# A decoder layer on one core: all four pooling groups computed ahead of the attention, and the output projection of the first 256 tokens placed inside the last head pair

## The chip, the cores and the metric

One core of one Trainium2 chip runs the whole layer. The metric is the device time of one execution in microseconds. Three executions of the kernel before took 1055.33, 1055.5 and 1056.11 us; the median is 1055.5 us.

## The reference

One layer over 1024 tokens (S) of width 1024 (D), all in float32. `h = x @ w_in` gives four pooling groups of 128 columns, queries, keys and values of eight heads of 64 columns, and eight forget logits.

```
pool = scale * GroupLinear(TrailingMean_w(u) - u)     w = 2, 4, 8, 16 for the four groups
attn = causal softmax(q k / 8 + c_t - c_s) v          c = cumsum(log sigmoid(f + b_f))
x    = LayerNorm(alpha * x + concat(pool, attn) @ w_out)
x    = LayerNorm(alpha * x + relu(x @ w_mlp1)^2 @ w_mlp2)
```

## The kernel before, in words

**Precision.** Every float32 matrix is split into a rounded part "hi" and a remainder "lo" (`split`: line 71 is the cast on ScalarE, line 72 the subtraction on VectorE), and a product is three matmuls, hi*hi, hi*lo and lo*hi (`three`, lines 83 to 85). "Fill" below means matmuls of lines 83 to 85 of 512 columns.

**Stages.** Values and forget logits of all tokens; the pooling groups 3, 2, 1 (`EARLY`), whose projection is 48 fill matmuls each (`pool_group`), with 6 more in `pool_linear`; keys and queries of head pair 0 (`qk_proj`); then the attention, four pairs of heads; then the output projection and first LayerNorm of eight blocks t of 128 tokens; then the MLP, written as block products over quarters of the tokens (line 575, second matrix line 918).

**Attention.** A unit is (pair p, head e, token block m of 256 queries). `att_probs` makes scores in PSUM (lines 339, 340, and 342 for the mask), takes their running minimum with the gate row on VectorE (line 345) and the exponential on ScalarE (line 347). `att_values` transposes the probabilities on TensorE (line 368), splits each transposed tile (369 on ScalarE, 370 on VectorE), multiplies by the values (384), and joins the two halves (389 on ScalarE, 390 on VectorE). The result goes to `mix_dram` in HBM, unnormalised; `row_scales` (lines 399 to 404) sends the reciprocal row sums to `rin_dram`. The values of a unit are issued behind the scores of the next one.

**Fill inside the attention.** Between these steps `fillstep` issues pieces of three fill matmuls: in pairs 0 to 2 the projection of the next pair's keys and queries (96 matmuls), in pair 3 pooling group 0 (`LATE`, 54 matmuls). In pair 3 the units run by m, both heads for each, so that the first tokens are complete early.

**Output projection.** For each m the mixture is loaded back in two halves (pooling columns, attention columns), the second half is multiplied by the broadcast reciprocals (line 725), both are split; 48 matmuls make each block t, all eight k-tiles for columns 0 to 511 first, then for the rest. The norm runs on VectorE (`Norm.on_vector`), with one Sqrt on ScalarE (line 498). The normalised block is transposed (line 551) one block later.

**What sets the order.** Each engine runs its own list in order; the framework's scheduler writes these lists from the program and may move an instruction past others that it does not depend on. Buffers are slots of five tags (S 3, U 2, B 14, Q 10, A 9), and PSUM has banks s 3, pt 2, pv 1, mm 2. All loads and most stores go through the SP queue in order.

Of the kernel before, what the change touches and what calls it, by code (L numbers as in the profile page):

```python
# [8 lines left out]
F32 = mybir.dt.float32  # L9
# [3 lines left out]
ALU = mybir.AluOpType  # L13
# [16 lines left out]
EPS = 1e-5  # L30
MASK = -1e30
BIG = 3e38
EARLY, LATE = (3, 2, 1), (0,)


@with_exitstack
def trunk(ctx, tc, xT, xn, wuqk, wvf, bf, poolw, pscale, wout, g1, b1, w1, w2, g2, b2, out):
# [198 lines left out]
    def run(gen):  # L236
        for _ in gen:
            pass
# [29 lines left out]
    def pool_linear(g, slots):  # L268
        st = slot("S", [P], F32)
        nc.sync.dma_start(st, poolw[:, g])  # L270
        pw = slot("U", [2, P])
        split(pw[:, 0], pw[:, 1], st)
        dh, dl = pooled[g]
        mx = slot(slots, [S], F32)
        for c in range(NCH):
            cs = slice(c * CH, (c + 1) * CH)
            dst = bank("mm" if g in LATE else None)
# [4 lines left out]
    for g in EARLY:  # L282
        run(pool_group(g, None, "A"))
        if g == EARLY[0]:
            gate_sum(neglog)


# [118 lines left out]
    g0 = qk_proj(0)  # L406
    for _ in range(2 * KT):
        next(g0)
    pool_linear(EARLY[0], "A")
    run(g0)  # L410

    def last_fill():
        for g in LATE:
            yield from pool_group(g, "mm")
            pool_linear(g, "Q")

    fill = {"gen": iter(()), "credit": 0.0, "rate": 0.0}

    def fillstep():
        fill["credit"] += fill["rate"]  # L420
        while fill["credit"] >= 1.0:
            fill["credit"] -= 1.0
            next(fill["gen"], None)

    pend = None
    for p in range(NPAIR):
        if p + 1 < NPAIR:
            order = [(p, e, m) for e in range(2) for m in range(4)]
            gen, pieces, over = qk_proj(p + 1, "mm"), 4 * KT + 1, 28
        else:  # L430
            order = [(p, e, m) for m in range(4) for e in range(2)]
            gen, pieces, over = last_fill(), (2 * KT + 2) * len(LATE), 14
        fill.update(gen=gen, credit=0.0, rate=pieces / over)
        for unit in order:
            prob = att_probs(*unit)
            if pend is None:
                for g in EARLY[1:]:
                    pool_linear(g, "A")
            fillstep()
            if pend is not None:  # L440
                att_values(*pend)
            pend = (*unit, prob)
        run(gen)
    att_values(*pend)

    x1_dram = dr.tile([NT, P, D], F32, name="x1_dram")


    hid_dram = dr.tile([NF // 2, P, 2, 7 * CH], F32, name="hid_dram")
    H = KT // 2
    GROUPS = (("A12", "A11"), ("S1", "S2"), ("S3", "S4"), ("A22",))  # L460
    AT = {g[0]: 2 * i * CH for i, g in enumerate(GROUPS)}

    def quarters(a):
        return a.rearrange("p (q t) -> p q t", q=4)

    wo = []
    for kp in range(KT // 2):
        hi, lo = slot("B", [2, D]), slot("B", [2, D])
        for k in range(2):
            st = slot("S", [D], F32)  # L470
            nc.sync.dma_start(st, wout[2 * kp + k])
            split(hi[:, k], lo[:, k], st)
            wo.append((hi[:, k], lo[:, k]))

    def load_row(tag, src):
        t = slot(tag, [D], F32)
        nc.sync.dma_start(t, src.to_broadcast([P, D]))
        return t

    class Norm:  # L480

# [54 lines left out]
    gam, bet = load_row("Q", g1), load_row("Q", b1)  # L536
    A = {b: (slot("B", [H, CH]), slot("B", [H, CH])) for b in ("A11", "A12")}
    R0, R1, A22, raw22 = {}, {}, {}, {}

# [172 lines left out]
    NU = NF // 2  # L712
    units = [Unit(u) for u in range(NU)]
    last = None
    for m in range(4):
        mh = []
        for half in range(2):
            mf = slot("S", [4, 256], F32)
            nc.sync.dma_start(mf, mix_dram[m, :, 4 * half : 4 * half + 4, :])
            if half:  # L720
                rb = slot("S", [NPAIR, 256], F32)
                for e in range(2):
                    rows = rin_dram[e::2, m * 256 : (m + 1) * 256].rearrange("(o p) t -> o p t", o=1)
                    nc.sync.dma_start(rb[e * HD : (e + 1) * HD], rows.to_broadcast([HD, NPAIR, 256]))
                nc.vector.tensor_tensor(mf, mf, rb, ALU.mult)
            hi, lo = slot("Q", [4, 256]), slot("Q", [4, 256])
            split(hi, lo, mf)
            mh.append((hi, lo))
        for t in (2 * m, 2 * m + 1):
            ts_ = slice((t % 2) * P, (t % 2 + 1) * P)  # L730
# [10 lines left out]
            for n, part in enumerate(yp):  # L741
                ns = slice(n * CH, (n + 1) * CH)
                for k in range(KT):
                    a = mh[k // 4]
                    three(part, (a[0][:, k % 4, ts_], a[1][:, k % 4, ts_]), (wo[k][0][:, ns], wo[k][1][:, ns]), k == 0, k == KT - 1)
            if last is not None:
                x1_transposed(*last)
            nm = Norm(xt, gam, bet, x1_dram[t])
            for i, c in enumerate(nm.cols):
                nc.vector.scalar_tensor_tensor(xt[:, c], xt[:, c], ALPHA, yp[i], ALU.mult, ALU.add)  # L750
                nm.stats(i)
            nm.on_vector()
            last = (t, xt)

    def block(name, src):
# [55 lines left out]
    VERSIONS = ("B11", "B21", "T2", "T1", "T3", "B22", "T4")  # L811
    c0, c1 = slice(0, CH), slice(CH, D)
    tt = nc.vector.tensor_tensor
    y, k3s, t2b, rows = {}, {}, {}, {}

    class Pair:
# [188 lines left out]
    for i, x in enumerate(chain):  # L1005
        if isinstance(x, Unit):
            if x.u >= 4:
                at(i - 1, 0, x.load_f)
                at(i - 1, 2, x.load_g)
                at(i - 1, 3, x.split_f)  # L1010
                at(i - 1, 4, x.sums)
                at(i - 1, 6, x.split_t2)
            if x.u >= 3:
                at(i, 1, x.split_t14)
                at(i, 4, x.split_t3b)
            if x.kept is None:
                at(i + 1, 7, x.sums_s)
                at(i + 2, 1, x.out_r)
                at(i + 2, 2, x.out_s)
            else:  # L1020
                at(i + 1, 5, x.out_a)
                at(i + 1, 6, x.sums_s, x.out_r)
                at(i + 1, 7, x.out_s)
        else:
            for k, p in enumerate(p for p in pairs if FIRST[p.u] == x.s):
                if p.u == ORDER[0]:
                    at(i - 2, 1, p.load_f)
                    at(i - 2, 2, lambda p=p: p.load_g("Q"))
                else:
                    at(i - 1, 4 * k, p.load_f)  # L1030
                    at(i - 1, 2 + 3 * k, p.load_g)
                at(i - 1, 3 + 3 * k, p.split_b)
                at(i - 1 + k, 4 - 3 * k, p.sums)
                at(i - 1 + k, 5 - 4 * k, p.split_t2)
                at(i, 2 + k, p.split_t13)
                at(i, 6, p.split_t4b)
            if x.first:
                at(i - 1, 4, x.room)
            if 5 <= x.s < 13:
                at(i - 1, 6, x.load_x)  # L1040
                at(i, 4, x.add_x)
            for n, place in enumerate((-4, -1, 0, 2) if 2 <= x.s < 5 else (-2, 0, 2, 4)):
                at(i + (place < 0) * -1, place % 7, lambda x=x, n=n: x.load(GROUPS[n]))
            if x.s == NS - 5:
                at(i + 1, 0, lambda: rows.update(gb=(load_row("S", g2), load_row("S", b2))))
    at(1, 1, second.out_s)

    def places(i, n):
# [59 lines left out]
```

## Time and profile before

| | |
|---|---|
| median of three executions | 1055.5 us |
| the profiled execution | 1056.57 us, of which the span of its instructions 1054.8 us |
| TensorE / VectorE / ScalarE busy | 97% / 72% / 49% of the span |
| granted TensorE clock, mean | 0.991 |

A TensorE row of the profile counts an instruction from its start to its modelled end, and consecutive ones overlap; what a matmul costs in a stream is the distance from one start to the next. So a TensorE that is shown as busy may still be slower than its stream rate, and the comparison that helps is of a stretch's length with the number of its matmuls times that distance. Times inside the trace are counted from the start of the span.

### The profile page before, as it was taken

How to read it: one execution, taken by the hardware profiler on the slowest of the kernel's cores; microseconds unless marked ns; L12 is line 12 of the kernel's file. 1: busy time of each engine (PE TensorE's matmuls, PEld its weight loads, DVE VectorE, ACT ScalarE, POOL GpSimd, SP SyncE). 2: the span in 40 equal slices, each digit the busy share in tenths (PEclk: the TensorE clock that was granted, in tenths of full speed). 3: DMA queues.
4: the chain of work that ended last, by engine and by line, in shares of the span. 5: the costliest groups of instructions: out<-in, count | busy, mean ns of one | idle time of the engine just before them, and what ended most of it. 6: DMA issues, size and time to landing. Idle time of an engine off the chain costs nothing.

```text
span 1054.8 us, 14034 instructions
## 1 busy us (share of the span) xinstructions
PE 1023.5 (97%) x5006; PEld 847.5 (80%) x5006; DVE 761.3 (72%) x1297; ACT 513.6 (49%) x822; POOL 119.0 (11%) x187
## 2 busy tenths in 40 slices
PE   8999999999989999899999999999999999999995
PEld 8988787888768878688888888888788888888883
DVE  4576678676896798869878878788875566566446
ACT  4423565565773322567676666777621221122153
POOL 0000000000000021212212112120100000000056
PEclk9999999999999999899999999999999999999997
DMA  6202311111445542138756757665999888868753
GB/s 221 103 27 90 115 50 31 31 53 49 130 153 165 180 160 80 42 118 320 287 211 265 267 214 279 230 245 205 325 321 311 286 263 288 271 202 277 232 185 120
DMA packets 111510, 195.28 MB, mean 185 GB/s; under 512 B 9224, under 2 KB 77640, under 8 KB 111440
## 3 DMA queue, kind: packets, MB, share of 16 engines
q1 hardware_dynamic: 95456, 136.19, 39.5%
q0 software_dynamic: 15984, 58.20, 14.3%
q8 instruction: 39, 0.64, 0.3%
q14 instruction: 31, 0.25, 0.1%
HBM read 126.65 MB, written 67.70 MB: 184 GB/s over the span
## 4 chain that ended last, share of the span: by engine, by line
PE 83%; DVE 7%; DMA 4%; ACT 3%; issue 2%; SPq 0%; DVEq 0%; ACTq 0%
PE s L918 15%; PE s L575 12%; PE pv L918 8%; PE mm L575 7%; PE pt L575 6%; PE pv L575 4%; PE pv L384 3%; PE mm L85 2%; PE mm L83 2%; DMA S<-rin_dram 2%; PE mm L84 2%; PE s L83 2%; PE s L85 2%; PE s L84 2%; PE pt L918 2%
## 5 line engine op out<-in xcount | busy, mean ns | idle before, releaser
L71 ACT CAST B<-S 128x1024 fp32r<-128x1024 f32 (+1 forms) x92 | 78.5, 870 | 175.8 <-DMA S<-in_w_dram 70.3
L575 PE MATMUL s<-B,Q 128*128 128x512 f32 x504 | 121.8, 395 | 0.4 <-ACT B L71 0.4
L72 DVE TENSOR_TENSOR B<-S,B 128x1024 fp32r<-128x1024 f32 (+1 forms) x92 | 90.4, 994 | 39.8 <-ACT B L71 39.5
L575 PEld LDWEIGHTS s<-B,Q 128*128 128x128 f32 x504 | 96.2, 191 | 21.5 <-ACT B L71 0.9
L918 PE MATMUL s<-B,Q 128*128 128x512 f32 x399 | 96.9, 389 | 0.0
L71 ACT CAST Q<-S 128x1024 fp32r<-128x1024 f32 x53 | 55.6, 1051 | 66.8 <-PE s L575 17.9
L918 PEld LDWEIGHTS s<-B,Q 128*128 128x128 f32 x399 | 74.9, 188 | 15.6
L918 PE MATMUL s<-B,A 128*128 128x512 f32 x333 | 83.3, 395 | 3.8 <-DVE rt L499 2.2
L72 DVE TENSOR_TENSOR Q<-S,Q 128x1024 fp32r<-128x1024 f32 x53 | 64.6, 1221 | 25.7 <-ACT Q L71 25.5
L918 PEld LDWEIGHTS s<-B,A 128*128 128x128 f32 x333 | 62.6, 189 | 18.7 <-DVE rt L499 2.6
L575 PE MATMUL mm<-B,Q 128*128 128x512 f32 x324 | 77.6, 389 | 0.0
L693 POOL DMA_DIRECT2D hid_dram<-A x90 | 48.4, 543 | 233.9 <-ACT A L690 198.5
L575 PEld LDWEIGHTS mm<-B,Q 128*128 128x128 f32 x324 | 60.7, 188 | 12.9 <-DVE Q L72 0.4
L575 PE MATMUL pt<-B,Q 128*128 128x512 f32 x288 | 68.7, 389 | 0.0
L384 PE MATMUL pv<-A,B 128*128 128x256 f32 x320 | 61.6, 297 | 5.1 <-ACT A L369 3.3
L384 PEld LDWEIGHTS pv<-A,B 128*128 128x128 f32 x320 | 49.1, 188 | 21.4 <-ACT A L369 9.9
L575 PEld LDWEIGHTS pt<-B,Q 128*128 128x128 f32 x288 | 54.0, 188 | 11.2
L370 DVE TENSOR_TENSOR A<-pt,A 128x512 fp32r<-128x512 f32 (+1 forms) x80 | 49.2, 634 | 16.4 <-ACT A L369 15.8
L347 ACT ACTIVATE A<-A,nm 128x128 f32<-128x128 f32 (+3 forms) x64 | 49.8, 778 | 20.7 <-DVE nm L345 20.4
L691 DVE TENSOR_TENSOR A<-A,A 128x1024 f32<-128x1024 f32 x45 | 53.4, 1218 | 0.0
L83 PE MATMUL mm<-B,B 128*128 128x512 f32 x120 | 51.7, 431 | 0.0
L918 PE MATMUL pv<-B,Q 128*128 128x512 f32 x204 | 50.1, 389 | 0.0
(397 smaller groups left out, 2250.1 us busy)
## 6 DMA issues: line engine op xcount, KB each, us to landing
hid_dram<-A POOLq DMA_DIRECT2D x105, 512.0 KB, 4.0
S<-in_w_dram SPq DMA_DIRECT2D x62, 512.0 KB
Q<-hid_dram SPq DMA_DIRECT2D x104, 256.0 KB
A<-hid_dram SPq DMA_DIRECT2D x76, 256.0 KB
S<-in_wuqk_dram SPq DMA_DIRECT2D x12, 512.0 KB
A<-ncf_dram SPq DMA_DIRECT2D x8, 512.0 KB
S<-in_wout_dram SPq DMA_DIRECT2D x8, 512.0 KB
S<-mix_dram SPq DMA_DIRECT2D x8, 512.0 KB
```

Of the source, the lines that this page charges most:

```text
L71: nc.scalar.copy(hi, src)
L72: nc.vector.tensor_tensor(lo, src, hi.bitcast(F32), ALU.subtract)
L83: nc.tensor.matmul(dst, a[0], b[0], start=first, stop=False)
L84: nc.tensor.matmul(dst, a[0], b[1], start=False, stop=False)
L85: nc.tensor.matmul(dst, a[1], b[0], start=False, stop=last)
L347: nc.scalar.activation(pt[:, :nk], pt[:, :nk], AF.Exp, bias=nm, scale=-1.0, accum_out=rsum[h][:, i : i + 1])
L370: nc.vector.tensor_tensor(tt[:, 1, ev], tp[:, ev], tt[:, 0, ev].bitcast(F32), ALU.subtract)
L384: nc.tensor.matmul(ov, V[j][:, h].rearrange("p s d -> p (s d)"), tt[:, s, a:b], start=(j == 0 and s == 0), stop=(j == 2 * m + 1 and s == 1),)
L575: nc.tensor.matmul(dst, b[x][:, k], A[a][y][:, k], start=first and k == 0 and i == 0, stop=k == H - 1 and i == 2, skip_group_check=not first,)
L691: nc.vector.tensor_tensor(x, x, hi.bitcast(F32), ALU.subtract)
L693: nc.gpsimd.dma_start(hid_dram[self.u, :, i, AT[name] : AT[name] + 2 * CH], part.rearrange("p q n t -> p (q n t)"))
L918: nc.tensor.matmul(dst, h[:, p_], w[q_], start=first and u == self.us[0] and j == 0, stop=u == self.us[-1] and j == 2, skip_group_check=no ...
```

## The change

`GROUPED` replaces `EARLY` and `LATE`: all four pooling groups are projected ahead of the attention; the small products of groups 3 and 2 stand inside `qk_proj(0)`, those of 1 and 0 in the first unit. In pair 3 the fill is now the output projection of blocks t = 0 and 1 (96 matmuls and two norms). The output weights (`wo`), the norm's rows and the two x blocks take the B slots that the transposed input frees in pair 2. For every block the order is now half by half: pooling columns for both 512-column results, then attention columns for both.

```
-EARLY, LATE = (3, 2, 1), (0,)
+GROUPED = (3, 2, 1, 0)
...
+    def out_rows(t, yp):
+        ts_ = slice((t % 2) * P, (t % 2 + 1) * P)
+        for half in range(2):
+            for n, part in enumerate(yp):
+                for k in range(4):
...
+                    three(part, (a[0][:, k, ts_], a[1][:, k, ts_]), (w[0][:, ns], w[1][:, ns]), half + k == 0, half + k == 4)
+                    yield
...
+    def last_fill():
+
+        for t in range(2):
+            yp = [bank("mm") for n in range(2)]
+            yield from out_rows(t, yp)
+            first_norm(t, x01[t], yp)
...
-            gen, pieces, over = last_fill(), (2 * KT + 2) * len(LATE), 14
+            gen, pieces, over = last_fill(), 4 * KT + 2, 23
+            load_wo(0)
+            mixed(0, 0)
+            load_wo(1)
+            gb, x01 = slot("B", [2, D], F32), slot("B", [2, D], F32)
...
+                if pend[:3] == (NPAIR - 2, 1, 3):
+                    load_wo(2)
+                if pend[:3] == (NPAIR - 1, 0, 0):
+                    load_wo(3)
+                if pend[:3] == (NPAIR - 1, 1, 0):
+                    mixed(0, 1)
...
-    for m in range(4):
-        mh = []
+    x1_transposed(0, x01[0])
+    last = (1, x01[1])
+    for m in range(1, 4):
         for half in range(2):
...
+            mixed(m, half)
...
-                for un in units[:2]:
+                for un, tag in zip(units, ("B", "Q")):
                     un.load_f()
-                    un.split_f("B")
+                    un.split_f(tag)
```

`mixed(m, half)` and `load_wo(kp)` hold the loads and splits that stood inline before; `first_norm` holds the residual sum, the statistics and the norm.

Three places in the order. First TensorE in pair 3 of the kernel before, where its fill runs out: mm_3011 is pooling group 0, pt_3170 and pv_3169 belong to unit (3,1,1), pt_3261 to (3,0,2), the s tiles are scores.

```order
L84 MATMUL mm_3011<-B_415,B_2893 128x512
L85 MATMUL mm_3011<-B_415,B_2893 128x512
L368 MATMUL pt_3170<-ident_63,A_3076 128x128
L339 MATMUL s_3159<-Q_2283,Q_2284 128x256
...
L384 MATMUL pv_3169<-A_3179,B_379 128x256 x2
L401 MATMUL pt_3229<-ident_63,ri_3227 2x128
L384 MATMUL pv_3169<-A_3179,B_379 128x256 x2
L368 MATMUL pt_3261<-ident_63,A_3140 128x128
```

From there to the middle of unit (3,0,3) only six fill matmuls follow. The same place in TensorE's list of the change: mm_3100 is the second result of block t = 0, pt_3164 belongs to unit (3,1,0), pv_3222 to (3,0,1), pv_3373 to (3,0,2).

```order
L85 MATMUL mm_3100<-B_2975,Q_2972 128x512
L368 MATMUL pt_3164<-ident_63,A_3091 128x128
...
L384 MATMUL pv_3222<-A_3232,B_379 128x256 x2
L368 MATMUL pt_3297<-ident_63,A_3200 128x128
...
L83 MATMUL mm_3099<-B_3070,Q_3196 128x512
L84 MATMUL mm_3099<-B_3071,Q_3196 128x512
L83 MATMUL mm_3100<-B_3070,Q_3196 128x512
L84 MATMUL mm_3100<-B_3071,Q_3196 128x512
L384 MATMUL pv_3373<-A_3419,B_445 128x256 x2
L401 MATMUL pt_3449<-ident_63,ri_3447 2x128
L85 MATMUL mm_3099<-B_3070,Q_3197 128x512
```

The 24 fill matmuls of the pooling half of t = 0 come first; then none, from unit (3,1,0) to the end of (3,0,2); then Q_3196 and Q_3197, the attention half of the mixture, are there, and 38 stand nearly in a block. Last, ScalarE's list of the change behind that point: rt_3392 is the norm of t = 0, pt_3487 and pt_3495 are transposed probabilities of unit (3,1,2), A_3546 are scores of (3,1,3).

```order
L71 CAST Q_3763<-S_3757 128x1024
L431 ACT_TABLE_LOAD
L431 ACTIVATE rt_3392<-mv_3391,eps_77 128x1
L369 CAST A_3488<-pt_3487 128x512
L369 CAST A_3496<-pt_3495 128x512
...
L403 COPY row_3543<-pt_3541 2x128
L347 ACT_TABLE_LOAD
L347 ACTIVATE A_3546,rsum_3081<-A_3546,nm_3556 128x896
```

Before, one table load stood behind the last exponential; now the Sqrt of t = 0 lies between exponentials and that of t = 1 behind the last, so there are three table loads in place of one.

## Rows read from the trace of the kernel before

**Rows 1.** Busy time by stretch: start:end, length, busy us (instructions) of each engine, PEclk, DMA
```profile
50.00:100.00 50.00, 50.00 (x246) 42.09 (x245) 34.77 (x73) 13.47 (x23) 0.00 (x0) 1.00 0.17 58
...
165.00:218.00 53.00, 52.45 (x317) 42.80 (x316) 39.54 (x95) 33.38 (x73) 2.50 (x8) 1.00 0.14 41
...
271.00:294.00 23.00, 22.53 (x133) 17.91 (x132) 19.59 (x46) 17.20 (x41) 1.25 (x4) 1.00 0.46 150
294.00:318.00 24.00, 19.59 (x128) 15.74 (x126) 21.76 (x55) 19.92 (x39) 0.94 (x3) 1.00 0.47 149
318.00:330.00 12.00, 11.17 (x68) 9.52 (x68) 8.98 (x12) 6.17 (x13) 0.31 (x1) 1.00 0.51 144
...
366.00:371.00 5.00, 4.13 (x21) 3.19 (x19) 4.50 (x10) 3.51 (x6) 0.00 (x0) 1.00 0.00 2
```
**Rows 2.** TensorE's groups in pair 1, 165 to 218: shape, count, busy, mean ns
```profile
L384 PE MATMUL pv<-A,B 128*128 128x256 f32 x80 | 14.9, 297 | 0.5 <-ACT A L369 0.3
L83 PE MATMUL mm<-B,B 128*128 128x512 f32 x32 | 13.9, 435 | 0.0
```
**Rows 3.** TensorE's groups from 271 to 330
```profile
L384 PE MATMUL pv<-A,B 128*128 128x256 f32 x96 | 18.8, 301 | 3.6 <-ACT A L369 2.4 <-DVE U L390 0.7 <-DVE A L370 0.2
L368 PE MATMUL pt<-ident,A 128*128 128x128 f32 x86 | 12.9, 274 | 0.9 <-ACT row L403 0.9
L83 PE MATMUL mm<-B,B 128*128 128x512 f32 x15 | 6.5, 431 | 0.0
...
L83 PE MATMUL s<-B,Q 128*128 128x512 f32 x9 | 3.7, 415 | 0.1
```
**Rows 4.** Chain that ended last: start, us, what; streams of matmuls at full rate
```profile
168.95 0.44 PE pt L368 x4
169.39 0.47 PE pv L384 x4
...
419.20 2.75 PE s L575 x12
```
**Rows 5.** TensorE's timeline: start, us, instruction, idle time before it and what ended it
```profile
301.73 0.47 PE L339 MATMUL s<-Q,Q 128*128 128x512 f32 x1 [1.02 <-DVE nm L345]
...
315.62 0.50 PE L384 MATMUL pv<-A,B 128*128 128x256 f32 x2 [1.13 <-ACT A L369]
...
370.63 0.63 PE L551 MATMUL pv<-ident,A 128*128 128x128 f32 x4 [0.87 <-DVE A L516]
```
**Rows 6.** VectorE's groups by shape, 272 to 325
```profile
L72 DVE TENSOR_TENSOR B<-S,B 128x1024 fp32r<-128x1024 f32 x8 | 9.7, 1216 | 2.1 <-ACT B L71 2.0
L370 DVE TENSOR_TENSOR A<-pt,A 128x512 fp32r<-128x512 f32 x13 | 8.6, 685 | 1.0 <-ACT A L369 1.0
L345 DVE CUSTOM_DVE_ANT_0 A<-s,A 128x512 f32<-128x512 f32 x10 | 6.8, 684 | 0.3 <-issue 0.2
...
L725 DVE TENSOR_TENSOR S<-S,S 128x1024 f32<-128x1024 f32 x1 | 1.2, 1225 | 1.2 <-DMA S<-rin_dram 1.2
```
**Rows 7.** VectorE's timeline: one norm of a block
```profile
406.58 0.69 DVE L750 SCALAR_TENSOR_TENSOR A<-A,pt 128x512 f32<-128x512 f32 x1 [2.62 <-PE pt L85]
...
409.77 2.43 DVE L513 SCALAR_TENSOR_TENSOR A<-A,mv,Q 128x512 f32<-128x512 f32 x2
...
412.82 1.42 DVE L516 SCALAR_TENSOR_TENSOR A<-A,rt,Q 128x512 f32<-128x512 f32 x2
```
**Rows 8.** ScalarE's timeline: the one table load behind the attention
```profile
339.14 1.05 ACT L71 CAST Q<-S 128x1024 fp32r<-128x1024 f32 x1 [9.42 <-DVE S L725]
340.20 1.28 ACT L498 ACT_TABLE_LOAD   x1
341.71 0.29 ACT L498 ACTIVATE rt<-mv,eps 128x1 f32<-128x1 f32 x1 [0.22 <-DVE mv L495]
```
**Rows 9.** Chain that ended last: loads of the broadcast reciprocals, issue to landing
```profile
315.70 5.84 DMA S<-rin_dram
...
330.94 6.81 DMA S<-rin_dram
```

More of the change, by code (lines that the diff above doesn't have):

```diff
@@ L280, in pool_linear @@
         nc.sync.dma_start(mix_dram[:, :, g, :].rearrange("m p t -> p m t"), mx.rearrange("p (m t) -> p m t", m=4))
-    for g in EARLY:
+    for g in GROUPED:
         run(pool_group(g, None, "A"))
-        if g == EARLY[0]:
+        if g == GROUPED[0]:
             gate_sum(neglog)
@@ L408, in trunk @@
         next(g0)
-    pool_linear(EARLY[0], "A")
+    for g in GROUPED[:2]:
+        pool_linear(g, "A")
     run(g0)
[L412 to L431, printed above, removed]
-            gen, pieces, over = last_fill(), (2 * KT + 2) * len(LATE), 14
[L433 to L478, printed above, removed]
     class Norm:
@@ L534, in affine, with load_row, load_wo, mixed @@
             eng.dma_start(self.store, self.y)
-    gam, bet = load_row("Q", g1), load_row("Q", b1)
+    wo, mh = [], {}
+    def load_row(dst, src):
+        nc.sync.dma_start(dst, src.to_broadcast([P, D]))
+    def load_wo(kp):
+        hi, lo = slot("B", [2, D]), slot("B", [2, D])
+        for k in range(2):
+            st = slot("S", [D], F32)
+            nc.sync.dma_start(st, wout[2 * kp + k])
+            split(hi[:, k], lo[:, k], st)
+            wo.append((hi[:, k], lo[:, k]))
+    def mixed(m, half):
+        mf = slot("S", [4, 256], F32)
+        nc.sync.dma_start(mf, mix_dram[m, :, 4 * half : 4 * half + 4, :])
+        if half:
+            rb = slot("S", [NPAIR, 256], F32)
+            for e in range(2):
+                rows = rin_dram[e::2, m * 256 : (m + 1) * 256].rearrange("(o p) t -> o p t", o=1)
+                nc.sync.dma_start(rb[e * HD : (e + 1) * HD], rows.to_broadcast([HD, NPAIR, 256]))
+            nc.vector.tensor_tensor(mf, mf, rb, ALU.mult)
+        hi, lo = slot("Q", [4, 256]), slot("Q", [4, 256])
+        split(hi, lo, mf)
+        mh[m, half] = hi, lo
@@ new lines, in trunk, with fillstep @@
+    x1_dram = dr.tile([NT, P, D], F32, name="x1_dram")
+    x01 = []
+    def last_fill():
[3 more added lines that the diff above has]
+            first_norm(t, x01[t], yp)
+    fill = {"gen": iter(()), "credit": 0.0, "rate": 0.0}
+    def fillstep():
+        fill["credit"] += fill["rate"]
+        while fill["credit"] >= 1.0:
+            fill["credit"] -= 1.0
+            next(fill["gen"], None)
+    pend = None
+    for p in range(NPAIR):
+        if p + 1 < NPAIR:
+            order = [(p, e, m) for e in range(2) for m in range(4)]
+            gen, pieces, over = qk_proj(p + 1, "mm"), 4 * KT + 1, 28
+        else:
+            order = [(p, e, m) for m in range(4) for e in range(2)]
+            gen, pieces, over = last_fill(), 4 * KT + 2, 23
[3 more added lines that the diff above has]
+            gb, x01 = slot("B", [2, D], F32), slot("B", [2, D], F32)
+            for t in range(2):
+                nc.sync.dma_start(x01[:, t], xn[t])
+            load_row(gb[:, 0], g1)
+            load_row(gb[:, 1], b1)
+            x01 = [x01[:, t] for t in range(2)]
+        rate = pieces / over
+        fill.update(gen=gen, credit=(over - 28) * rate, rate=rate)
+        for unit in order:
+            prob = att_probs(*unit)
+            if pend is None:
+                for g in GROUPED[2:]:
+                    pool_linear(g, "A")
+            fillstep()
+            if pend is not None:
+                att_values(*pend)
+                if pend[:3] == (NPAIR - 2, 1, 3):
[4 more added lines that the diff above has]
+                    mixed(0, 1)
+            pend = (*unit, prob)
+        if p + 1 < NPAIR:
+            run(gen)
@@ L537, in trunk, with quarters @@
+    att_values(*pend)
+    run(gen)
+    hid_dram = dr.tile([NF // 2, P, 2, 7 * CH], F32, name="hid_dram")
+    H = KT // 2
+    GROUPS = (("A12", "A11"), ("S1", "S2"), ("S3", "S4"), ("A22",))
+    AT = {g[0]: 2 * i * CH for i, g in enumerate(GROUPS)}
+    def quarters(a):
+        return a.rearrange("p (q t) -> p q t", q=4)
     A = {b: (slot("B", [H, CH]), slot("B", [H, CH])) for b in ("A11", "A12")}
@@ L740, in trunk @@
             yp = [bank() for n in range(2)]
[L741 to L752, printed above, removed]
+            for _ in out_rows(t, yp):
+                pass
+            x1_transposed(*last)
+            first_norm(t, xt, yp)
             last = (t, xt)
@@ L1044, in trunk @@
             if x.s == NS - 5:
-                at(i + 1, 0, lambda: rows.update(gb=(load_row("S", g2), load_row("S", b2))))
+                at(i + 1, 0, lambda: rows.update(gb=[row_of("S", v) for v in (g2, b2)]))
     at(1, 1, second.out_s)
```

26 lines of the change are left out of this document (13 added, 13 removed).

## The prediction

> **What bounds the kernel now.** I read the busy times by stretch first. TensorE is the bound nearly everywhere, so the question of each stretch is how far TensorE falls behind its own stream. From the chain I took the stream distances: a transpose costs 0.11 us (four in 0.44), a value matmul of 256 columns 0.118 (four in 0.47), a fill matmul of 512 columns 0.227 (twelve in 2.72 to 2.75) [rows 4]; scores go at the rate of their columns. TensorE's floor in a stretch is the sum of these.
>
> Pair 1 takes 53.0 us [rows 1]. It holds 96 fill matmuls (32 on each of three lines) and 80 value matmuls [rows 2], 72 transposes, and 48 score matmuls of 256 to 512 columns with 16 small masks: 21.8 + 9.4 + 7.9 + 9.3 = 48.4 us. So 4.6 us are lost, 9.5% on top of the floor. VectorE is busy for 39.54 of 53 us there.
>
> The last pair and the joint behind it, 271 to 330, are 59 us [rows 1]. There stand 96 value matmuls and 86 transposes, and 77 fill matmuls (line 83 has 15 and 9 in its two large groups, 27 in all) [rows 3], with 44 score matmuls: 11.3 + 9.5 + 17.5 + 9.1 = 47.4 us. So 11.6 us are lost. They are lost where the fill has run out: from 294 to 318 TensorE is busy for 19.59 of 24 us and VectorE for 21.76, or 91% [rows 1], and the idle pieces end with results of VectorE and ScalarE [rows 5]. The reader should see that this stretch is VectorE's: attention units there wait for minima and evictions.
>
> After 330 TensorE streams, but for one piece: 0.87 us before the transposes of the third block, which wait for VectorE's norm [rows 1, 5].
>
> **The change part by part.** *Pooling group 0 moves ahead.* Its 54 fill matmuls, 12.3 us, leave pair 3 and come ahead of pair 0. There TensorE is busy for all of 50 us and VectorE for 34.77 [rows 1], so they cost their floor, no more and no less: zero in the sum. That cover, VectorE's 30% of free time, takes the group's sums.
>
> *96 matmuls of the output projection move into pair 3*, 21.8 us, out of a stretch where they ran at the floor. This is zero too; what can be gained is only part of the 11.6 us lost. The same holds for the new order of halves inside a block: as many matmuls, and the first result is finished 12 matmuls (2.7 us) before the second, enough for its residual sum and statistics, two passes of 0.69 us [rows 7].
>
> *What pair 3 loses now.* I cut the new list of TensorE into three stretches and gave each VectorE's work by row means.
> First, up to unit (3,1,0): 24 fill, 28 value matmuls, 21 transposes and scores, a floor of 13.4 us, against 11.0 us of VectorE. TensorE leads, and I take pair 1's 9.5%: 1.3 us lost.
> Second, from there to the end of (3,0,2), seven fill matmuls in all: 34 value matmuls, 28 transposes and 5.3 us of scores, a floor of 13.9 us. VectorE has 14 minima at up to 0.68 us and eight evictions at up to 0.69 us [rows 6], less about 0.07 of overlap each, four joins, four reciprocals, and one multiply and one split of the mixture at 1.2: 17.0 us. At the 91% of the stretch before this takes 18.7 us: 4.8 lost.
> Third, to the last values: 100 fill, 44 value matmuls, 41 transposes, six transposes of x1 and 1.8 us of scores, a floor of 34.8 us, of which 38 fill matmuls (8.6 us) stand nearly in a block and lose nothing. VectorE has two norms of 6.8 us (two sums and two statistics of 0.6, the two pairs of 2.4 and 1.4, and small ones [rows 7]), seven passes for the mixture at 1.2, eleven evictions and five minima: 33 us. The two are almost level. I take 9.5% on the other 26.2 us, 2.5, and 0.5 for waits at the norms (next point): 3.0 lost.
> Together 9.1 in place of 11.6: **a gain of 2.5 us**. Bounds: pair 1's 9.5% on all but the block gives 5.1 lost, a gain of 6.5; VectorE at 85% in the second stretch and in the third, its share from 271 to 294 [rows 1], gives 1.3 + 6.1 + 4.0, and with each norm holding TensorE for 2 us more 15.4, a loss of 3.8. I take a value near the 91% row since that is the nearest stretch of the same kind: the eight weight splits (9.7 us of VectorE [rows 6]) and the pooling sums that crowded it are now earlier or gone, but the units themselves still have no fill.
>
> *Norms and their Sqrt among the exponentials.* Two more table loads on ScalarE, each 1.28 us, the next instruction of ScalarE following after 0.22 us that are put down to VectorE [rows 8]: 2.6 us. ScalarE is busy for 83% of the worst stretch before [rows 1], so these hide, if the Sqrt behind them doesn't wait. It does wait in order: the Sqrt needs the statistics, these stand on VectorE behind a multiply (line 725 before) that needs a load of reciprocals, and that load takes 5.84 to 6.81 us [rows 9]. It is issued behind the store of unit (3,0,2); VectorE has some 6 us of other work by then. Before, VectorE waited 1.2 us for such a load [rows 6]. I take 0.5, and keep 0 and 2 per norm as bounds. Behind the waiting Sqrt queue the casts of transposed tiles, and TensorE waits for those.
> The Trainium skill, "ScalarE: Activation LUTs", section "What ACT_TABLE_LOAD costs", says that a switch costs 1283 ns and a drain of about 1380 ns, 2.66 us together, and that functions should be grouped by table set; by it ScalarE would lose 5.3 us and not 2.6. The trace agrees with the load's 1.28 us and shows no drain on either side: the load starts 0.01 us after the cast ends.
>
> *Weights and rows earlier.* Four of eight weight splits and one of the mixture, 6 us of VectorE and 5 of ScalarE, move into pair 2. VectorE goes from 39.5 to 45.6 of 53 us, 86%, about the share of 271 to 294, where TensorE's idle time is 2.0% against 1.0% in pair 1 [rows 1]. So I take 1.0% of 53: **a loss of 0.5 us**, bounds 0 and 1.5. On SP the gate row of head 7 now stands behind two weight loads and one that waits for a buffer; TensorE has about 12 us of work in hand there, so it costs nothing. The loads that go along (weights, norm rows and x blocks, 512 KB each, as many as before) meet DMA engines that are busy for 0.14 of pair 1 [rows 1].
>
> *The piece at 370* goes: the mixture of the last tokens is now multiplied and split earlier, and the transposes of the third block come 17 us behind the end of the attention. **A gain of 0.9 us**, bounds 0 and 1. The joint to the MLP keeps its order.
>
> Sum: 2.5 + 0.9 - 0.5 = 2.9 us, so 1053.7 from the profiled execution's 1056.57, which lies 1.07 above the median; 1052.6 beside the median of 1055.5. That is the forecast: **1052.6**.
>
> **The rivals.** *The idle time only moves* (no change). For it: both lists show a stretch of three to four units with no fill, bound by VectorE, and the change brings as much VectorE work as it moves away (two norms, 13.6 us, for sums and splits). Then 11.6 stay lost, and 0.9 less 0.5 is left: 1055.1.
> *The pair comes down to the others' rate* (larger gain). For it: weight splits and pooling sums leave the crowded stretch. Against it: no fill there. A gain of 6.5 + 0.9 - 0.5: 1048.6.
> *ScalarE stops at the Sqrt* (slower). If the reciprocals land 2 us late, VectorE's multiply, then ScalarE's table load, Sqrt and cast follow in a row before TensorE has its next tile: 2 + 1.28 per norm, twice, 6.6, less the 0.5 already counted. It decides from about 1.5 us of waiting per norm: 1052.6 + 6.1 = 1058.7. The Trainium skill's rule on grouping by table set, named above, would make this the case, its drain adding 2.7 us.
>
> **How the numbers follow.** A measurement can tell about 0.2%, 2.1 us. Forecast (1049.5 to 1053.4) 0.38; larger gain 0.08; idle only moves (1053.4 to 1057.6) 0.29; Sqrt or another in-order wait (above 1057.6) 0.25. So faster 0.46, same 0.29, slower 0.25. The forecast's own range is 1049.5 to 1053.4; the range for 8 in 10 reaches through both other cases, 1049.0 to 1059.0.
>
> **What would show it.** In the profile after: TensorE full in the 12 us added ahead of the attention; in pair 3 one stretch of about 19 us with VectorE above 85% and TensorE idle in pieces of a microsecond; no wait of 0.9 us in the block transposes. The gain is wrong if pair 2 grows by over 1.5 us, or if TensorE waits for line 369 behind a Sqrt; the slower rival shows as ScalarE idle ahead of line 431, with VectorE idle ahead of line 493 for a load of reciprocals.

## The result, and the profile after

The changed kernel is slower: 1058.86 us against 1055.72 us (medians of 8 executions each), a ratio of 1.0031 with a 95% interval of 1.0022 to 1.0040. The forecast was 1052.6. Timed once more, beside 29 executions of the kernel before, it took 1057.72 against 1055.88, 1.0017 (1.0008 to 1.0027). Single executions of it lie between 1055.8 and 1060.3, so one profile is one draw; there are two, and the difference between them is part of the answer.

The start difference of the same instruction in both kernels tells where time goes. "MLP1" and "MLP2" are the two MLP halves; the last two points before the span are the 247th and 1204th matmul of MLP2, whose rows stand with the first experiment.

| point | before | after, first profile | after, second profile |
|---|---|---|---|
| first score of pair 0 | 111.56 | 123.13 (+11.57) | 123.38 (+11.82) |
| first matmul of MLP1 | 418.96 | 419.24 (+0.28) | 417.48 (-1.48) |
| first matmul of MLP2 | 724.37 | 723.73 (-0.64) | 722.60 (-1.77) |
| 247th of MLP2 | 791.18 | 792.64 (+1.46) | 789.60 (-1.58) |
| 1204th of MLP2 | 1008.67 | 1011.99 (+3.32) | 1008.94 (+0.27) |
| span | 1054.8 | 1058.2 (+3.4) | 1055.2 (+0.4) |

Four things are to be read from it. From the first score to MLP1 12.3 us of fill are gone and 2.9 more were to be gained; the way is shorter by 11.3 us in the first profile and by 13.3 in the second. In MLP1 the first profile is 0.92 us shorter than before and the second 0.29, which is not put down to the change: behind a wait of 3.7 to 3.9 us near its head the clock falls in every profile of this study, and it falls for a shorter time in the first one (granted clock from 425 to 450: 0.86 before, 0.93 and 0.86 after). At the joint into MLP2 (first to 247th matmul) the first profile loses 2.10 us and the second 0.19. And then both lose the same 1.85 us, bit by bit, over 957 matmuls.

Before, then after:

```profile
425.00:450.00 25.00, 20.86 (x81) 15.97 (x80) 21.07 (x34) 12.70 (x21) 5.11 (x1) 0.86 0.19 64
```
```profile
425.00:450.00 25.00, 20.45 (x85) 15.90 (x84) 21.43 (x34) 13.42 (x21) 5.13 (x1) 0.93 0.21 73
```

The stretches of the first profile that answer to [rows 1] (start:end, length, busy us of TensorE, its weight loads, VectorE, ScalarE, GpSimd, granted clock, DMA share):

```profile
110.00:122.00 12.00, 12.00 (x55) 9.85 (x53) 6.08 (x11) 5.74 (x11) 0.00 (x0) 1.00 0.75 260
...
294.00:318.00 24.00, 21.71 (x127) 17.05 (x126) 21.28 (x58) 17.47 (x42) 1.25 (x4) 1.00 0.36 112
318.00:330.00 12.00, 10.20 (x48) 8.38 (x47) 8.01 (x16) 4.38 (x7) 0.00 (x0) 0.87 0.29 91
...
326.40:330.20 3.80, 3.80 (x15) 3.37 (x16) 3.15 (x7) 1.42 (x3) 0.00 (x0) 0.57 0.21 77
...
762.70:766.00 3.30, 3.27 (x10) 2.46 (x11) 3.30 (x6) 1.65 (x2) 0.00 (x0) 0.67 1.08 366
766.00:770.00 4.00, 4.00 (x16) 3.23 (x15) 0.89 (x2) 0.49 (x1) 0.00 (x0) 0.84 1.06 360
```

The moved pooling group fills TensorE (12.00 of 12.00). From 294 to 318 TensorE is busy for 21.71 us where it was 19.59; these are the same times, but not the same work. What is new is 318 to 330: 10.20 busy us in place of 11.17, and a granted clock of 0.87. Inside, from 326.40 to 330.20, it is 0.57: of the two levels, 1.2 and 2.4 GHz, mostly the lower. What stands ahead of it, in the chain that ended last (first row) and in the timelines of VectorE, ScalarE and TensorE (start, us, instruction, idle time before it and what ended it):

```profile
315.82 6.11 DMA S<-rin_dram
...
319.47 0.69 DVE L424 BATCH_NORM_STATS2 bns<-B 128x6 f32<-128x512 f32 x1
321.95 1.23 DVE L493 TENSOR_TENSOR S<-S,S 128x1024 f32<-128x1024 f32 x1 [1.78 <-DMA S<-rin_dram]
...
323.21 1.05 ACT L71 CAST Q<-S 128x1024 fp32r<-128x1024 f32 x1 [5.98 <-DVE S L493]
324.28 1.28 ACT L431 ACT_TABLE_LOAD   x1
325.58 0.29 ACT L431 ACTIVATE rt<-mv,eps 128x1 f32<-128x1 f32 x1
325.78 1.05 ACT L369 CAST A<-pt 128x512 fp32r<-128x512 f32 x2
...
326.40 0.50 PE L384 MATMUL pv<-A,B 128*128 128x256 f32 x2 [1.80 <-ACT A L369]
...
346.14 0.47 PE L384 MATMUL pv<-A,B 128*128 128x256 f32 x2 [1.44 <-DVE U L390]
...
344.38 1.23 DVE L493 TENSOR_TENSOR S<-S,S 128x1024 f32<-128x1024 f32 x1 [1.78 <-issue]
```

The rows down to 326.40 are one chain. VectorE waits 1.78 us for the reciprocals of the third and fourth token block, which the scheduler had placed ahead of the last attention units. ScalarE waits 5.98 us for VectorE's multiply, casts, loads a table, takes the Sqrt of t = 0, and only then evicts the transposed probabilities (line 369) that TensorE wants: 1.80 us idle. Behind it TensorE runs 3.8 us at 0.57, which costs an estimated 3.8 x 0.43 = 1.6 us more. In the second profile VectorE waits 1.15 us for the load, TensorE idles for 1.15, and the clock stays at 1.00. At 344 VectorE stands still once more ahead of such a multiply, for the fifth and sixth block; its row names no releaser, but the last landing event of that load in the trace, at 344.30, stands 0.08 us ahead of it. This time the join of line 390 is queued behind it, and TensorE idles for 1.44 us (1.62 in the second profile).

### The profile page after: what moved, and what is told of

Same layout as the page of the kernel before. It is cut to its first block, busy times and chain, and to the rows that moved or that the text cites. A ratio compares the mean times of both kernels' runs of the same rounds, so it can differ in the third digit from the quotient of the medians.

```text
span 1058.2 us, 14019 instructions
## 1 busy us (share of the span) xinstructions
PE 1025.3 (97%) x5006; PEld 848.0 (80%) x5006; DVE 760.7 (72%) x1297; ACT 517.2 (49%) x824; POOL 119.5 (11%) x187
## 4 chain that ended last, share of the span: by engine, by line
PE 86%; DVE 5%; DMA 3%; ACT 2%; issue 2%; SPq 0%; DVEq 0%; ACTq 0%
PE s L960 15%; PE s L629 11%; PE pv L960 8%; PE mm L629 7%; PE pt L629 6%; PE pv L629 4%; PE pv L384 3%; PE mm L85 3%; PE mm L83 3%; PE mm L84 3%; PE s L83 2%; PE s L85 2%; PE s L84 2%; PE pt L83 2%; PE pt L85 2%; PE pt L84 2%
## 5 line engine op out<-in xcount | busy, mean ns | idle before, releaser
L629 PE MATMUL mm<-B,Q 128*128 128x512 f32 x336 | 80.5, 389 | 0.0
L629 PEld LDWEIGHTS mm<-B,Q 128*128 128x128 f32 x336 | 63.0, 188 | 13.4 <-DVE Q L72 0.4
L369 ACT CAST A<-pt 128x512 fp32r<-128x512 f32 (+1 forms) x80 | 42.2, 540 | 19.2 <-PE pt L368 18.4
```

Of the source, the lines that this page charges most:

```text
L629: nc.tensor.matmul(dst, b[x][:, k], A[a][y][:, k], start=first and k == 0 and i == 0, stop=k == H - 1 and i == 2, skip_group_check=not first,)
```

## Experiments

Times are medians of 11 or 12 executions, unless said. Lines of the kernels with moved buffers stand 4 lines further down.

### The A buffers 192 bytes up, in both kernels

A steady drift with no idle time had no place in the prediction. The two kernels issue the same matmuls there; what differs is which A buffers hold the tiles. The A buffers are 4160 bytes apart, so they start at 224, 32, 96 and 160 bytes past a multiple of 256 in turn, while all Q and B buffers start 32 past. Before, the h tiles (the stationary operands) of MLP2 lie in A0, A1, A4, A5, A8; after the change, in A1, A2, A5, A6, A7, since the sums took the others.

```
             hi, lo = slot("A", ...)      # load_wvf, first A buffer
+        if kp == 0:
+            small([P, 48], "gap1")       # 192 bytes ahead of A
...
+        if c == 0 and kp == 0:
+            small([P, 16], "gap2")       # Q and B as far up as 256 bytes
```

> The changed kernel with all nine A buffers moved 192 bytes up in SBUF (nothing else moves, no instruction changes). Theory (where a stationary operand lies sets the matmul's rate): from the traces of both kernels, the second MLP half takes 226 to 227 ns per matmul with its stationary operand in a buffer that starts 32 bytes past a multiple of 256, 229 at 224 bytes past, 233 at 96 or 160 past. The changed kernel's h tiles lie in A1, A5 (32 past), A2, A6 (96) and A7 (160); moved, these are 224, 32 and 96 past. So 234 matmuls lose 2.4 ns, 207 gain 6.3, 108 stay: 0.7 us less, 1058.2 us, the drift behind 792 us falls from 2.07 to about 1.4 us, and streams of 12 matmuls on A of 2.96 us turn into 2.88. Rival (the drift has another cause, such as loads or VectorE's sums on those buffers): 1058.9, no stream changes its rate.

> The kernel before with its nine A buffers moved 192 bytes up. Its h tiles lie in A0, A4, A8 (224 bytes past a multiple of 256) and A1, A5 (32 past); moved, these are 160 and 224 past. Theory (place of the stationary operand): 321 matmuls go from 2.4 to 6.3 ns on top, 228 from 0 to 2.4, 12 from 6.3 to 0: 1.7 us more, 1057.4 us, with no change ahead of the second MLP half. Rival (addresses do nothing): 1055.7.

Measured: the changed kernel 1055.93 (ratio to before 1.0004, 0.9994 to 1.0013); the kernel before 1058.42 (1.0021, 1.0010 to 1.0032). Streams of 12 matmuls at the same two places of the program, in the timeline: before, then after, then after with A moved, then before with A moved.

```profile
913.92 2.91 PE L918 MATMUL pt<-B,A 128*128 128x512 f32 x12
...
922.12 2.88 PE L918 MATMUL s<-B,A 128*128 128x512 f32 x12
```
```profile
916.40 2.96 PE L960 MATMUL pt<-B,A 128*128 128x512 f32 x12
...
924.68 2.96 PE L960 MATMUL s<-B,A 128*128 128x512 f32 x12
```
```profile
912.80 2.88 PE L964 MATMUL pt<-B,A 128*128 128x512 f32 x12
...
920.98 2.96 PE L964 MATMUL s<-B,A 128*128 128x512 f32 x12
```
```profile
913.77 2.96 PE L922 MATMUL pt<-B,A 128*128 128x512 f32 x12
...
922.08 2.91 PE L922 MATMUL s<-B,A 128*128 128x512 f32 x12
```

The first stream's stationary tiles start 224 bytes past a multiple of 256 (2.91), then 96 (2.96), then 32 (2.88), then 160 (2.96); the second's 32 (2.88), 160 (2.96), 96 (2.96) and 224 (2.91). In these eight streams the price goes with the place. The drift is read between two streams, 957 matmuls apart: before 217.49 us, after 219.35 (219.34 in the second profile), after with A moved 218.27, before with A moved 219.82. (The expectations on record count 960, from six matmuls earlier to three earlier: 218.17, 220.01 and 218.95.)

```profile
791.18 2.00 PE L918 MATMUL pv<-B,A 128*128 128x512 f32 x8
...
1008.67 2.21 PE L918 MATMUL s<-B,A 128*128 128x512 f32 x9
```
```profile
792.64 2.02 PE L960 MATMUL pv<-B,A 128*128 128x512 f32 x8
...
1011.99 2.22 PE L960 MATMUL s<-B,A 128*128 128x512 f32 x9
```
```profile
789.62 1.98 PE L964 MATMUL pv<-B,A 128*128 128x512 f32 x8
...
1007.89 2.22 PE L964 MATMUL s<-B,A 128*128 128x512 f32 x9
```
```profile
789.78 1.79 PE L922 MATMUL pv<-B,A 128*128 128x512 f32 x7
...
1009.60 2.25 PE L922 MATMUL s<-B,A 128*128 128x512 f32 x9
```

So the theory holds in sign and place, and its sums are too low: 1.08 us of drift went where 0.7 was expected, and in the kernel before 2.33 came where 1.7 was, nearly all of the 2.5 us that it lost. What the difference is stays open. The rest of the changed kernel's 1.8 to 2.9 us is not shown to come from places: its profile has the piece at 326 us (1.67 us) at a full clock, as the second profile of the change has.

### The Sqrt later, and no reciprocals

Which link of the chain at 326 us decides? One kernel keeps the Sqrt of t = 0 and 1 behind the last exponential, another leaves out the late load.

```
+    eps2 = small([P, 1], "eps2")
+    nc.vector.tensor_scalar(eps2, rsum[NH - 1][:, NT - 1 : NT], 0.0, EPS / 4, ALU.mult, ALU.add)
+    for nm in late:                      # norms of t = 0, 1
+        nm.eps = eps2
+        nm.on_vector()
```

> The changed kernel with the Sqrt of the first two blocks' norms held until the last exponential of the attention, by a constant that VectorE makes from its row sums. Theory (ScalarE stops at the Sqrt): at 322 to 330 us a late load of reciprocals, a table load and a Sqrt stand ahead of the casts of transposed probabilities, TensorE idles for 1.80 us and then runs 3.8 us at a granted clock of 0.57, which costs 1.6 more. Without Sqrt and table load the cast starts some 1.5 us earlier, the idle piece falls to about 0.3 us and the clock stays: 3.1 to 3.4 us less, 1055.5 to 1055.8. Rival 1 (the late load of reciprocals alone decides): an idle piece over 1.2 us stays there, the clock falls again: 1058.5. Rival 2 (VectorE bounds the pair, so the idle time moves to the next units): 1058.9 with the clock at 1.00.

```
-        if half:
+        if half and m != 1:
             rb = slot("S", [NPAIR, 256], F32)
```

> The changed kernel without the load of reciprocals and the multiply for the third and fourth token block (their attention part of the mixture stays unscaled; everything else, the Sqrt between the exponentials too, stays). Theory (the late load decides, and table load and Sqrt only lengthen its chain): without it VectorE passes from the second statistics at 320.2 us straight to the norm, ScalarE's table load and Sqrt are over before the transposes at 322.6 us end, TensorE's piece of 1.80 us there falls below 0.3 us and the clock stays at 1.00: 1.8 to 3.4 us less, and 1.2 us of VectorE besides, 1055.4 to 1057.1. Rival (the Sqrt and its table load by themselves stop ScalarE): over 1.2 us of idle time stays there, 1058.5 or more.

Measured: Sqrt late 1055.71 (0.9993, 0.9984 to 1.0002), as the theory said; no reciprocals 1054.92 (0.9992, 0.9984 to 1.0001), 0.5 below its range. ScalarE and TensorE with the Sqrt late, then ScalarE and the stretch without the load:

```profile
325.15 1.05 ACT L71 CAST Q<-S 128x1024 fp32r<-128x1024 f32 x1 [5.83 <-DVE S L494]
326.10 1.07 ACT L369 CAST A<-pt 128x512 fp32r<-128x512 f32 x2
...
326.73 0.51 PE L384 MATMUL pv<-A,B 128*128 128x256 f32 x2 [0.25 <-ACT A L369]
```
```profile
317.03 1.28 ACT L431 ACT_TABLE_LOAD   x1
319.60 0.29 ACT L431 ACTIVATE rt<-mv,eps 128x1 f32<-128x1 f32 x1 [1.28 <-DVE mv L428]
...
318.00:330.00 12.00, 12.00 (x66) 9.73 (x65) 9.80 (x22) 5.18 (x10) 0.32 (x1) 1.00 0.14 51
```

Either cure removes the piece at 326. Without Sqrt and table load the casts of line 369 follow the late cast at once, and 0.25 us of idle time is left. Without the load the table load and the Sqrt are over before TensorE's transposes are, and TensorE is busy for all of 12 us. The second piece, behind line 390, is gone with the Sqrt late and 1.15 us long without the one load. So at 326 neither Sqrt nor load alone stops TensorE: each hides, and their sum, in one in-order queue, does not.

### The changed kernel once more

No edit.

> The changed kernel itself once more, for a second profile. Theory: the idle piece of about 1.8 us at 326 us and the long wait at 762 us are in it again, each followed by a stretch at a lower granted clock; median 1058.9. Rival (the falls of the clock are accidents of single executions, not of this kernel): in the second profile one or both stay away, and the span is 1.5 to 3 us shorter.

```profile
326.06 0.50 PE L384 MATMUL pv<-A,B 128*128 128x256 f32 x2 [1.15 <-ACT A L369]
...
761.24 1.77 PE L960 MATMUL s<-B,A 128*128 128x512 f32 x6 [1.81 <-DMA A<-hid_dram]
```

Both pieces are there, both falls of the clock are not, and the span is 3.0 us shorter. So the pieces belong to the kernel, and these two falls to single executions. In the first profile the wait at the joint is 1.99 us and the clock falls behind it (0.67, then 0.84); before, it comes in three parts with the clock at 1.00:

```profile
762.73 2.16 PE L960 MATMUL s<-B,A 128*128 128x512 f32 x6 [1.99 <-DMA A<-hid_dram]
```
```profile
760.52 0.96 PE L918 MATMUL s<-B,A 128*128 128x512 f32 x3 [0.41 <-DMA A<-hid_dram]
...
762.51 0.97 PE L918 MATMUL s<-B,A 128*128 128x512 f32 x3 [1.03 <-DMA A<-hid_dram]
763.70 0.94 PE L918 MATMUL s<-B,A 128*128 128x512 f32 x3 [0.22 <-DMA A<-hid_dram]
```

The joint waits for loads while the DMA engines' share is 1.06. A lead in front of it need not be lost there: the kernel without the late load comes to MLP2 5.4 us ahead of before, and its first 247 matmuls take 66.48 us, against 66.81 before.

### Only the pooling group ahead

```
-EARLY, LATE = (3, 2, 1), (0,)
+EARLY, LATE = (3, 2, 1, 0), ()
```

> The kernel before with only the pooling group moved ahead of the attention, and no fill in the last pair. My prediction's step (the moved 54 matmuls cost their floor of 12.3 us ahead, and pair 3 loses what it lost): 1055.7. Theory: pair 3 without fill is VectorE's and comes down by less than 12.3 us, so 2 to 4 us slower ahead of the MLP; and its h tiles of the second MLP half lie in A3, A7 (160 bytes past a multiple of 256, 222 matmuls), A0-like ones (224 past, 216) and A1, which costs 1.1 us more than before's: together 1058.8 to 1060.8. If places in SBUF do nothing, 1057.7 to 1059.7.

Measured: 1059.37 (5 executions; 1.0036, 1.0023 to 1.0050), in the range of the theory, but also in the range named for places that do nothing. Of the 3.5 us above before, 1.7 are the drift of its own places in MLP2 (219.17 us for the 957 matmuls), which leaves 1.8 for the move. The profiled execution took 1061.36; there 2.8 us are lost at the first matmul of MLP2 (727.13 in place of 724.37). Most of it is lost at the end of pair 2, where VectorE is busy for 4.91 of 5 us with evictions, a weight split and the passes over the last queries; TensorE idles for 2.60 us and the clock falls:

```profile
280.00:285.00 5.00, 3.36 (x27) 2.94 (x25) 4.91 (x9) 3.87 (x7) 0.31 (x1) 1.00 0.77 285
285.00:290.00 5.00, 3.07 (x10) 2.13 (x10) 4.23 (x12) 3.01 (x7) 0.00 (x0) 0.68 0.06 16
...
285.96 0.36 PE L339 MATMUL s<-Q,Q 128*128 128x256 f32 x1 [2.60 <-DVE nm L345]
```

### The mixture on GpSimd

A cure that leaves nothing out: the late multiply and split off VectorE and ScalarE, alone and with the Sqrt late.

```
-            nc.vector.tensor_tensor(mf, mf, rb, ALU.mult)
+            (nc.gpsimd if m == 1 else nc.vector).tensor_tensor(mf, mf, rb, ALU.mult)
...
+        if half and m == 1:
+            nc.gpsimd.tensor_copy(hi, mf)
+            nc.gpsimd.tensor_tensor(lo, mf, hi.bitcast(F32), ALU.subtract)
```

> The changed kernel with the multiply by the reciprocals and the split of the third and fourth token block's mixture on GpSimd in place of VectorE and ScalarE. Theory (VectorE and ScalarE stop in order behind that late load): they no longer pass it, so the idle piece at 326 us falls below 0.3 us and the clock stays, as without the load (1054.9): 2.3 to 2.8 us less than the changed kernel's 1057.7 to 1058.9, so 1055.0 to 1056.5. GpSimd's three passes of 2.4 us end some 7 us behind the load, at about 329, ahead of their first use. Rival: the wait moves to GpSimd's zero fills of transposed tiles, which queue behind the passes: an idle piece over 1 us behind GpSimd, 1058.

> Both cures of the piece at 326 us together: the third and fourth block's mixture on GpSimd, and the Sqrt held until the last exponential. Theory (one chain of load, cast, table load and Sqrt): the second cure adds nothing to the first but one table load less, 1054.8 to 1056.2. Rival (Sqrt and table load cost of their own behind VectorE): 1 us or more below the kernel with the mixture on GpSimd alone.

Measured: alone 1057.20 (1.0012, 1.0001 to 1.0023), with the Sqrt late 1055.16 (0.9993, 0.9985 to 1.0002). The first misses the theory and the second sides with its rival, but by another way than the rival named. Alone (GpSimd, VectorE, TensorE; the profiled execution took 1060.05):

```profile
324.44 2.40 POOL L493 TENSOR_TENSOR S<-S,S 128x1024 f32<-128x1024 f32 x1 [14.45 <-DVE rt L436]
...
324.97 3.85 DVE L449 SCALAR_TENSOR_TENSOR B<-B,rt,B 128x512 f32<-128x512 f32 x2
328.75 1.28 DVE L370 TENSOR_TENSOR A<-pt,A 128x512 fp32r<-128x512 f32 x2
...
329.48 0.75 PE L384 MATMUL pv<-A,B 128*128 128x256 f32 x2 [2.20 <-DVE A L370]
```

The norm's last two passes, 1.40 us together in the changed kernel, took 3.85 beside GpSimd's multiply and cast, and the evictions behind them came 2.4 us late. With the Sqrt late those passes come later, no longer beside GpSimd, and TensorE is busy from 318 to 330 without a gap. The Trainium skill, "GPSIMD Engine Reference", section "Specifications", says that GpSimd shares its SBUF interfaces with VectorE and that instructions of VectorE with two SBUF inputs contend; the trace agrees with its 3.85 us against 1.40. With the Sqrt late, two evictions that have one input in PSUM ran beside GpSimd's passes and took 1.29 us, as elsewhere.

### Places for A

A fourth position of A, then the Sqrt held together with the first move.

> The changed kernel with its A buffers moved 224 bytes up: A1 and A5 start at a multiple of 256, A2 and A6 64 past, A7 128 past. A look at streams of 12 matmuls with a stationary operand in A behind 792 us. Theory (32 past a multiple of 256 is the best place, each other place has its price): 2.88 to 2.96 us for all of them. Rival (a multiple of 256 is better still): A1 and A5 below 2.88, which would pay for Q and B too, where all buffers start 32 past.

```profile
915.21 2.95 PE L964 MATMUL pt<-B,A 128*128 128x512 f32 x12
...
923.52 2.97 PE L964 MATMUL s<-B,A 128*128 128x512 f32 x12
```

Places 64 and 128 past a multiple of 256 (these two rows) and 0 past (2.96 in another stream) all cost as much as 96 and 160; 32 past is the best of those seen. One execution took 1059.33.

> The changed kernel with both: Sqrt held until the last exponential, A buffers 192 bytes up. If the two effects are separate they add: 3.15 us (Sqrt) and 1.06 us (drift from the joint on, 276.38 in place of 277.44 us) less than 1058.86: 1054.6, faster than both kernels. If the 2.9 us that the move of A alone gave came mostly from the same idle piece at 326 us, only the drift is added, the same number; if the two stand for the same cause altogether, 1055.7.

Measured: 1055.93 (0.9997, 0.9987 to 1.0007), a miss: no sum of the two. Its drift is the moved kernel's to 0.01 us and its piece at 326 is 0.39 us. But in its profile TensorE waits at two places where the kernel with the late Sqrt alone did not:

```profile
343.83 0.48 PE L388 MATMUL pv<-A,B 128*128 128x256 f32 x2 [0.99 <-DVE U L394]
...
381.83 0.63 PE L619 MATMUL s<-ident,A 128*128 128x128 f32 x4 [0.79 <-DVE A L454]
```

The first is the piece behind line 390 again, which is between 0 and 1.6 us long in the profiles of this study. The kernel with the mixture on GpSimd and the Sqrt late has both as well (0.80 us at 342 and 0.57 at 379) with A where the change has it, so the move of A is not needed for them. What brings them in some executions stays open.

Last, more of MLP2's sums and fewer of its h tiles in A, and A 64 bytes up; with the mixture on GpSimd and the Sqrt late, and on the change alone.

```
-                y[t] = slot("Q" if self.q < 2 else "A", [D], F32)
+                y[t] = slot("Q" if self.q < 1 else "A", [D], F32)
...
-                h = slot("A" if nh[0] % 11 > 5 else "Q", [per, 2, n, P])
+                h = slot("A" if nh[0] % 11 > 8 else "Q", [per, 2, n, P])
```

> The last kernel, with the second MLP half's tiles placed for TensorE: six of the eight sums in A in place of four, two of eleven h loads in A in place of five, A 64 bytes up, so that of 1344 matmuls 72 have a stationary operand 224 bytes past a multiple of 256 and all others 32 past. Theory (place): from the 96th matmul behind the joint on, 960 matmuls in place of 220.0 us (218.95 with A 192 bytes up) take 217.0 to 217.5: 2.5 to 3 us less than the same kernel without it, 1052.0 to 1053.5, faster than both kernels. Rival (fewer free buffers for h make TensorE wait for loads): the distances fall to 227 ns, but idle pieces behind loads take 1 us or more of it.

> The changed kernel with the places of the last kernel alone (sums and h tiles of the second MLP half, A 64 bytes up), Sqrt and mixture as the change has them. Theory (places and the piece at 326 us are separate terms): the drift is gone as in the last kernel (960 matmuls in 217.7 us, against 220.0 of the changed kernel and 218.2 of before), 2.3 us less than the changed kernel's 1057.7 to 1058.9: 1055.4 to 1056.6, level with before; the piece at 326 us stays, 1.1 to 1.8 us long. Rival (the last kernel owed its gain to the two cures, and fewer buffers for h eat up the places): 1057.5 or more.

Measured: with the cures 1053.44 (0.9979, 0.9969 to 0.9988), faster than both kernels; places alone 1056.15 (0.9998, 0.9988 to 1.0008), level with before. Both as the theory said. The 957 matmuls take 1006.35 - 789.31 = 217.04 us, 2.3 less than in the change:

```profile
743.58 0.96 PE L978 MATMUL pv<-B,B 128*128 128x512 f32 x3 [2.15 <-ACT A L986]
...
789.31 1.98 PE L978 MATMUL pv<-B,Q 128*128 128x512 f32 x8
...
1006.35 2.66 PE L978 MATMUL s<-B,Q 128*128 128x512 f32 x11
```

The rival has a part, by another way than loads of h: with more sums in A, ScalarE waits for a store that frees an A buffer, and TensorE for 2.15 us at 743 behind it (1.68 with the places alone). The waits for h at 760 are gone.

## Why the prediction was wrong

*Pooling group 0 ahead costs its floor*: right in place (12.00 of 12.00 us, first score 11.6 us later where 12.3 were counted, a point that stands between 122.5 and 124.8 in the profiles of the change and its variants). That it costs nothing as a whole holds only with other fill in pair 3; alone it lost about 1.8 us by the medians and 2.8 ahead of MLP2 in the profile.

*96 matmuls move into pair 3 at their floor*: right in the block from 318.78 to 322.41, where sixteen distances are 0.227 us each; behind the waits of the next points it does not hold. *Earlier weights cost pair 2 0.5*: it cost nothing; the last value matmuls of pairs 0, 1 and 2 stand 11.6, 11.6 and 11.5 us behind those of before.

*What pair 3 loses now, 9.1*: too low. Cut as there, and with the distances of [rows 4], the stretches took 15.2, 19.9 and 40.5 us for floors of 12.9, 13.9 and 33.7: lost 2.3, 6.0 and 6.8 in place of 1.3, 4.8 and 3.0. The first two are the same in every profile of the change and its variants (15.2 to 15.7 and 19.8 to 20.0). The third is where the profiles differ: 38.5 us in the second one, and with the Sqrt held as many matmuls of nearly the same kinds take 35.6 (alone), 35.8 (with the mixture on GpSimd), 35.6 (with the places too) and 36.9 (with A 192 bytes up). That is some 2 us lost in the first three, where 2.5 were forecast without waits at the norms; the excess of the change is the next term. These ends are not those of the stretch of before, so the balance is the table's. From the first score to MLP1, beyond the 12.3 us of fill that left, the change lost 1.0 us in the first profile and gained 1.0 in the second, where 2.9 were forecast; the four kernels with the Sqrt held, in the order above, gained 2.7, 2.2, 3.0 and 0.8.

*0.5 for waits at the norms*: this is the term that was mis-sized. The mechanism stood in the text, step by step: a Sqrt behind statistics behind a multiply behind a load of reciprocals, with the casts for TensorE queued behind. The two late loads cost TensorE 1.15 + 1.62 us in one profile and 1.80 + 1.44 in the other, and there 1.6 more by the granted clock, which had not been counted: 2.8 to 4.8 in place of 0.5, above the bound of 2 per norm once the clock falls. Holding the Sqrt back gave 2.0 to 3.2 us on the change, and nothing on top of the moved A buffers (1055.93 with and without). The step that failed is "VectorE has some 6 us of other work by then": from the issue of the load at 315.82 to the end of VectorE's last instruction ahead of the multiply, 320.16, are 4.3 us, the load took 6.11, inside the 5.84 to 6.81 of [rows 9], and VectorE waited the 1.78 between. In the second profile it was 4.4, 5.48 and 1.15. The wait of 1.2 us that the prediction read for such a load before was the better guide. The slower rival, 1058.7, named this mechanism, and its sign came as written: ScalarE idle ahead of line 431, VectorE idle ahead of line 493 for the reciprocals. That its number came so near is luck, since 1.85 us of what was measured stand in MLP2, where it has none; and its table load counts at t = 0 alone. At t = 1 the Sqrt stands behind the last exponential, and the load stops VectorE by itself.

The Trainium skill, "ScalarE: Activation LUTs", section "Rules for kernel authors", says to group functions by table set, and here moving the Sqrt of the first blocks paid on the change. The drain of some 1380 ns that its section "What ACT_TABLE_LOAD costs" adds to a load is not in the trace: the load took 1.28 us, ending at 325.56, and the Sqrt starts at 325.58.

*The piece at 370 goes*: right; from 354.4 to 372 TensorE is busy for 17.60 of 17.60 us.

*Not in the sum at all*: MLP2. The change renames which A buffers are free there, and 1.85 us of drift follow in both profiles (219.34 us as well in the four kernels that leave the places of the change as they are, 217.04 with good places); in the first, 1.9 more at the joint. The prediction followed the instructions of a moved step to all engines and queues, but not the buffers that it holds.

The two terms are of the size that the balance needs. With the late Sqrt, the mixture on GpSimd and good places (1053.44) the change is 2.5 us faster than before, about the 2.9 that the prediction saw in it; the Sqrt in its place costs 2.0 to 3.2 and the places 1.6 to 2.7, and the change stands 1.8 to 3.1 above before. That they simply add is not shown: the late Sqrt with A 192 bytes up did not.

## What to carry to other kernels

Where a change moves allocations, compare which buffer each tile gets, also in stages far behind the edit. A small function of another table set between exponentials is cheap until a wait stands ahead of it in the same queue: add up the whole queue, not each link. And price an idle piece of a tight TensorE stream with the clock that may fall behind it; here that cost about as much again (1.6 us behind 1.80).

## What was unexpected of the hardware

A matmul of 128x512 with its stationary operand 32 bytes past a multiple of 256 in its partition comes every 226 ns, at 224 bytes past every 229, at 0, 64, 96, 128 or 160 past every 233 to 235 (2.88, 2.91 and 2.95 to 2.97 us for twelve, less 0.39 for the last, over eleven). Moving buffers by 192 bytes, with no instruction changed, moved a kernel's time by 2.5 us, 2.33 of them between the two streams of the second MLP half.

Two passes of VectorE with both inputs in SBUF took 3.85 us in place of 1.40 beside GpSimd's passes.

Of TensorE's idle pieces, those of 1.80 us at 326 and 1.99 us at 762 were followed by a lower granted clock in one execution, those of 1.15 and 1.81 at the same places in another were not. The length of the piece does not tell which: one of 1.87 us with the Sqrt late was followed by a fall, one of 2.04 with the mixture on GpSimd and the Sqrt late was not. The wait of 3.7 to 3.9 us in the first MLP half was, in all fourteen profiles.
